# Forty of 48 activation tiles copied by DMA and transposed as float32r

## The chip, the cores and the metric

One core of one Trainium2 chip runs the kernel. The metric is the device time of one execution in microseconds, as the median of several runs. The engines named below: TensorE (PE in the profile; its loads of the stationary operand have a row of their own, PEld), VectorE (DVE), ScalarE (ACT), GpSimd (POOL) and the queue SP, from which most transfers are started. PSUM is the memory that TensorE writes into; a bank holds 128 x 512 float32.

## The reference

One decoder layer for 256 rows of 2048 channels in float32: attention over selected keys and a retention branch side by side, merged by sigmoid gates, then an MLP with a squared ReLU. Cut to what matters here:

```python
h = rms_norm(x, ln1_g[l])
aq, ak, av, iq, ik, iw, rq, rk, rv, rg, ga, gb = split(h @ w_in[l])
o_attn = dsa_attention(aq, ak, av, iq, ik, iw, topk)
y_ret = retention_chunkwise(rq, rk, rv, log_gamma)
o_ret = silu(rg) * group_norm_heads(y_ret, ret_gn_g[l], ret_gn_b[l])
merged = sigmoid(ga) * (o_attn @ w_up_attn[l]) + sigmoid(gb) * (o_ret @ w_up_ret[l])
x = x + merged @ w_out[l]
h2 = rms_norm(x, ln2_g[l])
x = x + square(relu(h2 @ w_ff1[l])) @ w_ff2[l]
```

The hidden width is 8192.

## The kernel before

**Products.** Every matrix product of size is made three times in float32r (`products`, L401 to L407): the rounded part of the activation with the rounded part of the weight, with the weight's rest, and the activation's rest with the rounded weight. So each operand exists as a pair of float32r tiles, `hi` and `lo`. For weights `split` makes the pair: ScalarE copies the raw tile into `hi` (L359), VectorE subtracts `hi` from the raw tile into `lo` (L360). For some weights VectorE first adds two raw tiles (L349). The stationary operand is the activation's, 128 x 128; the weights stream past it, 512 columns at a time.

**Order.** The whole work is a list of items, `use`, written ahead of time; one item is two K chunks of 128. In `run_block` and `second` (the second MLP product) an item is 12 products, in `first` (the sums of a fast block scheme for the gates and for the first MLP product) it is 6. `weights` starts loads up to 8 items ahead (1 MB each, on SP's queue) and splits 2 items ahead, in one case 3.

**Side work.** What has to be done beside the products are Python generators in the list `work`; each `step()` moves every one of them up to its next `yield`. `run_block` steps once for each K chunk, `first` and `second` once for each item. The instructions go into the engines' queues in that order, and each queue is worked off in order.

**Transposition.** Activations come out with rows on partitions and have to be turned before they can be a stationary operand. `transpose_in` (L432) waits a number of steps (the argument `wait`: 2, or `W_GN` = 7 for retention), takes a PSUM bank (`psum_t`, two of them in the first part, one in the MLP), has TensorE transpose four 128 x 128 blocks of a 128 x 512 tile into it (L438, with the float32 identity `ident`), and calls `split_into`: ScalarE copies the bank into `hi` (L429), VectorE subtracts into `lo` (L430). It is called 48 times:

- 8 times for the retention output (`normed`, L988): 4 blocks of 512 channels x 2 row tiles. VectorE's last operation before it is L987.
- 8 times for the merged tiles (L1043), blocks i = 0 to 3 x 2 row tiles; VectorE's L1042 makes the tile. Blocks 0 and 1 are the ones begun early over three quarters of K (`PAIR`, `PARTS`).
- 32 times for the MLP's activations (`hidden`, L1157), 8 groups of 1024 hidden channels x 2 halves x 2 row tiles. ScalarE makes ReLU (L1143) and square (L1144) into a staging tile.

In the groups 1 to 7 of the MLP, `merged(g)` interleaves the `first` items of group g with the `second` items of group g-1. `first` ends with `put`, which squares the tiles and calls `hidden`, after products 4 (two tiles), 5 and 6 (one each). The result of `second` is scaled by ScalarE (L1217) and added to a sum in memory by a DMA of GpSimd's queue (L1218).

**Staging tiles.** `stage()` gives a 128 x 512 float32 tile out of two rings: every fourth from a ring of 2, the others from a ring of 6. A tile whose slot is still in use makes its first writer wait.

Of the kernel before, what the change touches and what calls it, by code (L numbers as in the profile page):

```python
# [10 lines left out]
F32 = mybir.dt.float32  # L11
F32R = mybir.dt.float32r
I32 = mybir.dt.int32
AF = mybir.ActivationFunctionType
# [3 lines left out]
P = 128  # L18
# [4 lines left out]
BN = 512  # L23
# [10 lines left out]
FG = 8  # L34
NG = DFF // (FG * P)
# [124 lines left out]
def block_kernel(ctx, tc, cst, rot, xt, gains, w, x, ret_gn_g, ret_gn_b, out):  # L160
    nc = tc.nc
# [3 lines left out]
    cp = ctx.enter_context(tc.tile_pool(name="cp", bufs=1))  # L165
# [23 lines left out]


    W_NORM, W_SOFT, W_GN = 3, 5, 7
    n_stg, n_mid, n_sm = 8, {"ep": 12, "e4": 20}, 24
    late = {"ep": ep, "stg": ep}
    n_stage = [0]

    def nm(s):
        uid[0] += 1
        return f"{s}_{uid[0]}"

    def stage(shape=(P, BN)):  # L200
        n_stage[0] += 1
        pool, bufs = (late["stg"], 2) if n_stage[0] % 4 == 0 and "stg" in late else (sp, n_stg - 2)
        return pool.tile(list(shape), F32, tag="stg", name=nm("stg"), bufs=bufs)

    def mid(shape, dtype=F32):
        return late["ep"].tile(list(shape), dtype, tag="mid", name=nm("mid"), bufs=n_mid[late["ep"].name])

    def small(w):
        return sp.tile([P, w], F32, tag="small", name=nm("small"), bufs=n_sm)

    def psum_t():
        return PS["pt"].tile([P, BN], F32, tag="pt", name=nm("pt"))

    def psum_a():
        return PS["pa"].tile([P, BN], F32, tag="pa", name=nm("pa"))

    def act_pair(slot):
        a = ap[slot].tile([P, DK, 2, S], F32R, tag="act", name=nm("act"))
        return a[:, :, 0, :], a[:, :, 1, :], a

    work = []
# [19 lines left out]
    ident = csb[:, C_ID:C_ID + P]  # L241
    cmk = csb[:, C_CM:C_CM + P]


    warm = cp.tile([P, P], F32, name="warm")
    nc.vector.memset(warm, 0.0)
    wps = psum_a()
    for _ in range(11):
# [140 lines left out]
    def run_block(key, act, before=None, ps=None, k0=0, k1=None):  # L389
        nk, n = B[key]  # L390
        ps = ps or [PS["pm"].tile([P, BN], F32, tag="pm", name=nm("pm")) for _ in range(T)]
        for k in range(k0, k1 or nk):
            if k % HC == 0:
                ws = weights((key, k // KC, k % KC // HC))
            if before:
                before(k)
            step()
            products(ps, [p[:, :n] for p in (ws[0][:, k % HC], ws[1][:, k % HC])], [act(k, t) for t in range(T)], k == 0, k == nk - 1)
        return [p[:, :n] for p in ps]
# [9 lines left out]
    def of(a):  # L409
        return lambda k, t: tuple(z[:, k, t * P:(t + 1) * P] for z in a[:2])  # L410


    def rsqrt(v, n, mul):

        a, y, u = small(n), small(n), small(n)
        nc.vector.tensor_scalar(a, v, mul, EPS, op0=ALU.mult, op1=ALU.add)
        nc.vector.tensor_scalar(y.bitcast(I32), a.bitcast(I32), -0.5, float(0x5F3759DF), op0=ALU.mult, op1=ALU.add)
        for _ in range(3):
            nc.vector.tensor_tensor(u, y, y, op=ALU.mult)
            nc.vector.scalar_tensor_tensor(u, u, -0.5, a, op0=ALU.mult, op1=ALU.mult)  # L420
            nc.vector.scalar_tensor_tensor(y, u, 1.5, y, op0=ALU.add, op1=ALU.mult)
        return y

    def split_into(act, k0, nk, t, ps):

        src = ps.rearrange("p (c i) -> p c i", c=nk)
        hi = act[0][:, k0:k0 + nk, t * P:(t + 1) * P]
        lo = act[1][:, k0:k0 + nk, t * P:(t + 1) * P]
        nc.scalar.activation(hi, src, AF.Copy)  # L429
        nc.vector.tensor_tensor(lo, src, hi.bitcast(F32), op=ALU.subtract)  # L430

    def transpose_in(act, k0, t, src, wait=2):  # L432

        for _ in range(wait):
            yield
        ps = psum_t()
        for c in range(4):
            nc.tensor.transpose(ps[:, c * P:(c + 1) * P], src[:, c * P:(c + 1) * P], ident)  # L438
        split_into(act, k0, 4, t, ps)


# [32 lines left out]
    def evict(dst, ps, t, func=AF.Copy):  # L474
        nc.scalar.activation(dst, ps, func, scale=rows[t])
# [70 lines left out]
    for i in range(3):  # L546
        ps = run_block(("I", i), of(hT)) if i else psI
        for t in range(T):
            evict(iqs[:, t, i * IN:(i + 1) * IN], ps[t], t)
    mb = []  # L550

    def indexer():
        ik2 = mid([P, T, 2, ID])
# [70 lines left out]
    ps = run_block(("AV", 0), of(hT))  # L624
# [68 lines left out]
    for j in range(NKV):  # L693
        ps = run_block(("AQ", j), of(hT))
# [83 lines left out]
    def scaled(b):  # L778

        assert late["X2 made"]  # L780
        late["scaled"] = b + 1
        z = late["X2"][:, b // 2, b % 2 * 4:b % 2 * 4 + 4]
        hi, lo = (hT[a][:, 4 * b:4 * b + 4, P:] for a in range(2))
        nc.scalar.activation(hi, z, AF.Copy)
        nc.vector.tensor_tensor(lo, z, hi.bitcast(F32), op=ALU.subtract)

    for which, key in ((0, "RQ"), (1, "RK")):
        for i in range(2):
            last = (which, i) == (1, 0)
            ps = run_block((key, i), of(hT), before=(lambda k: scaled(k // 4 - 1) if k in (4, 8, 12) else None) if last else None)  # L790
# [93 lines left out]
    for gate, u in ((z, u) for z in BESIDE for u in range(2)):  # L884
# [10 lines left out]
        for item in beside(gate, u):  # L895
# [7 lines left out]
            else:  # L903
                branch(item, of(oT if gate == "GA" else hT))
                i = item[0][1] - 2 * u
# [13 lines left out]
    rT = act_pair(1)  # L919
# [28 lines left out]
    def retain(j, gb, rv, sg, am):  # L948
        for _ in range(2):
            yield  # L950
        ys = []
        for t in range(T):
            psy = psum_a()
            for a in range(2):
                c = slice(a * RV, (a + 1) * RV)
                for u in range(t + 1):
                    m = slice((a * (T - u) + t - u) * P, (a * (T - u) + t - u + 1) * P)
                    products([psy[:, c]], [v[:, c] for v in rv[u]], [[z[:, m] for z in am[u]]], u == 0, u == t)
            y = stage()
            nc.scalar.activation(y, psy, AF.Copy)  # L960
            ys.append(y)
            yield
        yield from normed(j, ys, gb, sg)

    def normed(j, ys, gb, sg):
        mv, vr, nb = small(4 * T), small(2 * T), small(2 * T)
        for t in range(T):
            for a in range(2):
                st = small(6)
                nc.vector.bn_stats(st, ys[t][:, a * RV:(a + 1) * RV])  # L970
                nc.vector.bn_aggr(mv[:, 4 * t + 2 * a:4 * t + 2 * a + 2], st)
        mean, var = (mv.rearrange("p (a b) -> p a b", b=2)[:, :, i] for i in range(2))
        nc.vector.tensor_copy(vr, var)
        yield
        r = rsqrt(vr, 2 * T, 1.0)
        nc.vector.scalar_tensor_tensor(nb, mean, -1.0, r, op0=ALU.mult, op1=ALU.mult)
        yield
        for t in range(T):
            y = ys[t]
            for a in range(2):  # L980
                c = slice(a * RV, (a + 1) * RV)
                i = 2 * t + a
                nc.scalar.activation(y[:, c], y[:, c], AF.Identity, scale=r[:, i:i + 1], bias=nb[:, i:i + 1])
            nc.vector.tensor_tensor(y, y, gb[0], op=ALU.mult)
            nc.vector.tensor_tensor(y, y, gb[1], op=ALU.add)
            yield
            nc.vector.tensor_tensor(y, y, sg[t], op=ALU.mult)  # L987
            work.append(transpose_in(rT, 4 * j, t, y, W_GN))  # L988

    for j in range(4):  # L990
        if j < 2:

            i = j
# [5 lines left out]
        for src in (ret_gn_g, ret_gn_b):  # L999
            g = mid([P, BN])  # L1000
            nc.gpsimd.dma_start(g, src[:, j * BN:(j + 1) * BN].to_broadcast([P, BN]))
            gb.append(g)
        for t in range(T):
            z = mid([P, BN])
# [6 lines left out]
        ps = run_block(("RV", j), of(hT))  # L1011
# [9 lines left out]
    mT = act_pair(0)  # L1021
    pair = {}
    def gates(i):
        ms = [mid([P, BN]) for _ in range(T)]
        for t, m in enumerate(ms):
            nc.gpsimd.dma_start(m, mgd[:, t, i * BN:(i + 1) * BN])
            nc.gpsimd.dma_start(sgb[:, t, i * BN:(i + 1) * BN], sgbd[:, t, i * BN:(i + 1) * BN])
        return ms
# [7 lines left out]
    for i in range(4):  # L1036
        ms = mss[i] if i in pair else gates(i)
        ps = run_block(("UR", i), of(rT), ps=pair.get(i), k0=len(PARTS[0]) * KC if i in pair else 0)
        for t, m in enumerate(ms):
            g = sgb[:, t, i * BN:(i + 1) * BN]  # L1040
            nc.vector.tensor_tensor(g, ps[t], g, op=ALU.mult)
            nc.vector.tensor_tensor(m, m, g, op=ALU.add)  # L1042
            work.append(transpose_in(mT, 4 * i, t, m))  # L1043


    x2 = px.tile([P, T, D], F32, tag="big2", name="x2")
# [62 lines left out]
    for i in range(4):  # L1109
        ps = run_block(("O", i), of(mT))  # L1110
        for t in range(T):
            z = x2[:, t, i * BN:(i + 1) * BN]
# [13 lines left out]
    hid = act_pair(0)  # L1126
# [26 lines left out]
    def form(f, k):  # L1153
        return tuple(xf[:, a, f, k, :] for a in range(2))

    def hidden(g, t, i):
        work.append(transpose_in([z[:, g % 2 * FG:] for z in hid[:2]], 4 * i, t, ys.pop((t, i))))  # L1157

    blocks = ((X11, X21), (X12, X22))
    ys = {}  # L1160
    for i in (1, 0):
        ps = run_block(("F1", i), lambda k, t: form(blocks[k // HK][t], k % HK))
# [107 lines left out]
```

## Time and profile before

| | |
|---|---|
| median of 3 runs | 1610.87 us (1610.86 to 1611.2) |
| the profiled execution | 1610.98 us |
| its span, first to last instruction | 1609.2 us |
| mean granted TensorE clock | 1.000 |
| DMA moved | 351.80 MB, 219 GB/s |
| transpositions in `transpose_in` | 192 |

A profile row of the form `L438 PE MATMUL pt<-csb,stg ... x160` names the line, engine, operation, the tile written and the tiles read, the shape and the count. The names are those of tiles: `pt` is the PSUM bank of transpositions, `csb` holds the identity, `stg` are staging tiles, `whi` and `wlo` the weights' pair, `act` the turned activations' pair, `pm`, `pq`, `pf`, `pa` the banks of products. Both float32 and float32r operands of TensorE stand there as f32. In the chain, a line gives start, length and what ran; in a timeline the bracket at the end is the engine's idle time just before and what ended it.

### The profile page before, as it was taken

The page shows a single profiled execution, that of the slowest core. Times are in us where ns is not written, and L with a number is a line of the kernel's source. Part 1 is how long each engine was busy: PE and PEld are TensorE (multiplying, and loading weights), DVE is VectorE, ACT ScalarE, POOL GpSimd, SP SyncE. Part 2 cuts the span into 40 slices and gives each one's busy share as a digit, 9 for nine tenths or more (in the row PEclk, how much of TensorE's full clock was granted, in tenths as well). Part 3 has the DMA queues.
Part 4 walks back from the last instruction along what each step waited for, and adds up shares of the span by engine and source line. Part 5 has one row for each costly group of instructions (what it writes and reads, how often), then busy time and mean ns, then how long its engine had stood idle before and what let it go on. Part 6 is the DMA issues. An engine that isn't in the chain of part 4 may idle for free.

```text
span 1609.2 us, 19815 instructions
## 1 busy us (share of the span) xinstructions
PE 1603.2 (100%) x7438; PEld 1334.0 (83%) x7438; DVE 1308.5 (81%) x1466; ACT 1011.1 (63%) x1316; POOL 90.7 (6%) x135
## 2 busy tenths in 40 slices
PE   9999999999999999999999999999999999999999
PEld 8978888888888888888888888888888888888887
DVE  6678779898989898688665589898989898989884
ACT  7556666566566666455444666767767676767672
POOL 0000000000000001202000000000000000000000
PEclk9999999999999999999999999999999999999999
DMA  9645346656565655857556574767676777777773
GB/s 330 220 150 183 132 148 247 222 215 234 198 253 209 262 200 184 320 199 261 183 206 255 203 276 142 250 195 255 207 251 197 242 225 235 235 236 233 217 200 134
DMA packets 68416, 351.80 MB, mean 219 GB/s; under 512 B 7776, under 2 KB 14560, under 8 KB 32736
## 3 DMA queue, kind: packets, MB, share of 16 engines
q1 hardware_dynamic: 51040, 308.96, 52.6%
q0 software_dynamic: 14256, 35.14, 10.0%
q10 hardware_dynamic: 3024, 6.44, 1.1%
q8 instruction: 58, 0.95, 0.2%
q14 instruction: 38, 0.31, 0.1%
HBM read 323.24 MB, written 27.26 MB: 218 GB/s over the span
## 4 chain that ended last, share of the span: by engine, by line
PE 98%; DVE 1%; DMA 0%; ACT 0%; issue 0%; ACTq 0%; DVEq 0%
PE pm L407 12%; PE pm L406 12%; PE pm L405 12%; PE pf L405 11%; PE pf L407 11%; PE pf L406 11%; PE pq L406 9%; PE pq L405 9%; PE pq L407 9%; PE pt L438 1%; PE pa L405 1%; PE pa L407 0%; PE pa L406 0%; PE pt L532 0%; PE pt L681 0%; PE pa L940 0%
## 5 line engine op out<-in xcount | busy, mean ns | idle before, releaser
L360 DVE TENSOR_TENSOR wlo<-raw,whi 128x1024 fp32r<-128x1024 f32 (+2 forms) x544 | 646.3, 1201 | 214.8 <-ACT whi L359 205.3
L359 ACT ACTIVATE whi<-raw 128x1024 fp32r<-128x1024 f32 (+2 forms) x544 | 563.7, 1043 | 403.0 <-PE pm L407 193.2
L405 PE MATMUL pm<-whi,act 128*128 128x512 f32 (+1 forms) x800 | 310.0, 388 | 0.6 <-ACT act L449 0.6
L406 PE MATMUL pm<-wlo,act 128*128 128x512 f32 (+1 forms) x800 | 307.0, 384 | 0.5 <-DVE wlo L360 0.5
L407 PE MATMUL pm<-whi,act 128*128 128x512 f32 (+1 forms) x800 | 307.5, 384 | 0.0
L405 PE MATMUL pf<-whi,act 128*128 128x512 f32 (+1 forms) x768 | 298.7, 390 | 0.0
L406 PE MATMUL pf<-wlo,act 128*128 128x512 f32 (+1 forms) x768 | 298.4, 389 | 0.0
L407 PE MATMUL pf<-whi,act 128*128 128x512 f32 (+1 forms) x768 | 298.3, 388 | 0.0
L360 DVE TENSOR_TENSOR wlo<-rawc,whi 128x1024 fp32r<-128x1024 f32 x176 | 215.0, 1222 | 43.5 <-ACT whi L359 41.3
L359 ACT ACTIVATE whi<-rawc 128x1024 fp32r<-128x1024 f32 x176 | 186.4, 1059 | 81.2 <-PE pf L407 35.7
L349 DVE TENSOR_TENSOR raw<-raw,raw 128x2048 f32<-128x2048 f32 x88 | 201.2, 2287 | 1.3 <-DMA raw<-in_w_dram 0.6
L407 PEld LDWEIGHTS pm<-whi,act 128*128 128x128 f32 x800 | 150.5, 188 | 27.8 <-DVE act L450 0.2
L406 PEld LDWEIGHTS pm<-wlo,act 128*128 128x128 f32 x800 | 150.6, 188 | 26.9 <-DVE wlo L360 1.3
L405 PEld LDWEIGHTS pm<-whi,act 128*128 128x128 f32 x800 | 150.4, 188 | 26.9 <-ACT act L449 0.8
L405 PEld LDWEIGHTS pf<-whi,act 128*128 128x128 f32 x768 | 144.1, 188 | 30.1 <-ACT whi L359 0.8
L407 PEld LDWEIGHTS pf<-whi,act 128*128 128x128 f32 x768 | 144.3, 188 | 29.8
L406 PEld LDWEIGHTS pf<-wlo,act 128*128 128x128 f32 x768 | 144.3, 188 | 29.4
L405 PE MATMUL pq<-whi,xf 128*128 128x512 f32 x392 | 154.4, 394 | 0.0
L407 PE MATMUL pq<-whi,xf 128*128 128x512 f32 x392 | 152.9, 390 | 0.0
L406 PE MATMUL pq<-wlo,xf 128*128 128x512 f32 x392 | 152.7, 390 | 0.0
L1218 POOL DMA_DIRECT2D sums<-ev x56 | 48.2, 942 | 777.0 <-ACT ev L1217 775.3
L407 PEld LDWEIGHTS pq<-whi,xf 128*128 128x128 f32 x392 | 73.6, 188 | 15.4
(210 smaller groups left out, 1531.2 us busy)
## 6 DMA issues: line engine op xcount, KB each, us to landing
raw<-in_w_dram SPq DMA_DIRECT2D x188, 1024.0 KB, 5.3
rawc<-in_w_dram SPq DMA_DIRECT2D x88, 1024.0 KB, 5.8
sums<-ev POOLq DMA_DIRECT2D x56, 256.0 KB, 5.4
raw<-in_w_dram SPq DMA_DIRECT2D x8, 736.0 KB, 4.8
raw<-in_w_dram SPq DMA_DIRECT2D x7, 512.0 KB, 7.0
raw<-in_w_dram SPq DMA_DIRECT2D x8, 368.0 KB, 7.3
stg<-in_x_dram SPq DMA_DIRECT2D x8, 256.0 KB, 7.7
rqkd<-stg POOLq DMA_DIRECT2D x8, 256.0 KB, 2.7
```

Source lines behind the costliest of these rows:

```text
L349: nc.vector.tensor_tensor(one, one, two, op=ALU.add)
L359: nc.scalar.activation(a, src, AF.Copy)
L360: nc.vector.tensor_tensor(b, src, a.bitcast(F32), op=ALU.subtract)
L405: nc.tensor.matmul(d, h, hi, start=first, stop=False, skip_group_check=skip)
L406: nc.tensor.matmul(d, h, lo, start=False, stop=False, skip_group_check=skip)
L407: nc.tensor.matmul(d, l, hi, start=False, stop=last, skip_group_check=skip)
L438: nc.tensor.transpose(ps[:, c * P:(c + 1) * P], src[:, c * P:(c + 1) * P], ident)
L1218: nc.gpsimd.dma_start(sums[:, t, i * BN:(i + 1) * BN], z, accum_op=ALU.add)
```

## The change

`stage` can now give a float32r tile. `moved(src)` takes one and copies a finished 128 x 512 float32 tile into it by a DMA of ScalarE's queue, bit by bit (the destination is seen as float32). `transpose_in` turns a float32r tile with a float32r identity, `unit`, into the same PSUM bank seen as float32r, and any other tile as before. Retention's 8 calls, the 4 calls for merged blocks 0 and 1, and the 28 calls for the MLP's groups 0 to 6 go through `moved`; the 4 calls for merged blocks 2 and 3 and the 4 of the last MLP group stay as they are. The moved ones wait 10 steps (retention, merged tiles, half 1 of group 0) or 6 (the rest of the MLP), where they waited 7 and 2.

```diff
+    W_MOVED, W_EARLY = 6, 10
...
-    def stage(shape=(P, BN)):
+    def stage(shape=(P, BN), dtype=F32):
         n_stage[0] += 1
         pool, bufs = (late["stg"], 2) if n_stage[0] % 4 == 0 and "stg" in late else (sp, n_stg - 2)
-        return pool.tile(list(shape), F32, tag="stg", name=nm("stg"), bufs=bufs)
+        return pool.tile(list(shape), dtype, tag="stg", name=nm("moved" if dtype == F32R else "stg"), bufs=bufs)
+
+    def moved(src):
+
+        z = stage(dtype=F32R)
+        nc.scalar.dma_start(z.bitcast(F32), src)
+        return z
...
+    unit = cp.tile([P, P], F32R, name="unit")
...
+    def turn(ps, c, src, i):
+
+        d, z = ps[:, c * P:(c + 1) * P], src[:, i * P:(i + 1) * P]
+        if src.dtype == F32R:
+            nc.tensor.transpose(d.bitcast(F32R), z, unit)
+        else:
+            nc.tensor.transpose(d, z, ident)
+
     def transpose_in(act, k0, t, src, wait=2):
...
-            nc.tensor.transpose(ps[:, c * P:(c + 1) * P], src[:, c * P:(c + 1) * P], ident)
+            turn(ps, c, src, c)
...
+    nc.scalar.activation(unit, ident, AF.Copy)
...
-            work.append(transpose_in(rT, 4 * j, t, y, W_GN))
+            work.append(transpose_in(rT, 4 * j, t, moved(y), W_EARLY))
...
-            work.append(transpose_in(mT, 4 * i, t, m))
+            work.append(transpose_in(mT, 4 * i, t, *((moved(m), W_EARLY) if i < 2 else (m,))))
...
     def hidden(g, t, i):
-        work.append(transpose_in([z[:, g % 2 * FG:] for z in hid[:2]], 4 * i, t, ys.pop((t, i))))
+        y = ys.pop((t, i))
+        src = (moved(y), W_EARLY if i > 2 * g else W_MOVED) if g < NG - 1 else (y,)
+        work.append(transpose_in([z[:, g % 2 * FG:] for z in hid[:2]], 4 * i, t, *src))
```

## The prediction

> **What bounds the kernel now.** I read the page first: the busy shares, then the chain that ended last, by engine and by line.
>
> ```profile
> span 1609.2 us, 19815 instructions
> PE 1603.2 (100%) x7438; PEld 1334.0 (83%) x7438; DVE 1308.5 (81%) x1466; ACT 1011.1 (63%) x1316; POOL 90.7 (6%) x135
> ...
> PE 98%; DVE 1%; DMA 0%; ACT 0%; issue 0%; ACTq 0%; DVEq 0%
> ```
>
> TensorE works from end to end and 98% of the chain is TensorE. So a nanosecond taken out of TensorE's stream comes off the time, as long as no other engine falls behind. Next the transposition line, L438, and the table of waits for the weight loads.
>
> ```profile
> L438 PEld LDWEIGHTS pt<-csb,stg x160: 137/140/144, 690.7 to 1561.3; 128*128 128x128 f32 x160
> L438 PE MATMUL pt<-csb,stg x160: 269/272/328, 690.9 to 1561.4; 128*128 128x128 f32 x160
> L438 PE MATMUL pt<-csb,mid x32: 271/272/301, 789.8 to 841.4; 128*128 128x128 f32 x32
> ...
> PEld pt L438 <- ACT stg L1144: 1.9, 7, 0.4
> ...
> PEld pq L406 <- DVE wlo L360: 1.1, 4, 0.4
> ```
>
> 192 transpositions, four to a call. The 272 ns is the length of one from entry to exit, and they overlap; what one costs the stream has to be read from the chain in order of time (start, length, what).
>
> ```profile
> 145.52 0.89 PE pa L662 x8
> ...
> 668.49 0.86 PE pa L940 x4
> ...
> 673.29 0.12 PE pa L405
> 673.41 0.12 PE pa L406
> ...
> 690.87 0.23 PE pm L407
> 691.10 0.44 PE pt L438 x4
> 691.54 0.23 PE pm L405
> ...
> 1119.51 0.49 PE pt L438 x4
> ...
> 1122.08 0.44 PE pt L438 x4
> ```
>
> Four float32 transpositions hold the stream 0.44 us, 0.110 each. L662 is a plain float32 product of 128 columns and its records cost the same, 0.89/8 = 0.111; L940 with 256 columns costs 0.86/4 = 0.215. So a float32 record costs by its columns, 0.84 ns for each. The float32r products cost 0.12 at 256 columns and 0.23 at 512 (L405): 0.45 to 0.47 ns a column, about half.
>
> **Which transpositions change, counted from the code.** Retention output: 4 blocks x 2 row tiles = 8 calls. Merged tiles: blocks 0 and 1, 4 calls. MLP activations: 7 groups x 4 = 28. Together 40 calls, 160 transpositions; the last group and merged blocks 2 and 3 keep float32.
>
> **What a float32r transposition costs.** No row shows one, nor any float32r product of 128 columns. Two things can set it. The columns: half of the 0.12 is 0.060; a line through 0.12 and 0.23 also gives about 0.065; I take 0.064. The load of its 128x128 operand: here the timeline of the weight loads (start, length, line), and two rows by line with the mean and the median of one load in ns.
>
> ```profile
> 1119.34 0.14 PEld L438 LDWEIGHTS pt<-csb,stg 128*128 128x128 f32 x1 [0.25 <-ACT stg L1144]
> ...
> 1119.34 0.20 PEld L438 LDWEIGHTS pt<-csb,stg 128*128 128x128 f32 x2 [0.25 <-ACT stg L1144]
> ...
> 1119.73 0.19 PEld L405 LDWEIGHTS pq<-whi,xf 128*128 128x128 f32 x1
> 1119.84 0.19 PEld L406 LDWEIGHTS pq<-wlo,xf 128*128 128x128 f32 x1
> ...
> L405 PEld LDWEIGHTS pm<-whi,act 128*128 128x128 f32 x800 | 150.4, 188 | 26.9 <-ACT act L449 0.8
> ...
> L940 PEld LDWEIGHTS pa<-rqT,rk x32: 187/190/193, 665.4 to 722.0; 128*128 128x128 f32 x32
> ```
>
> In the answers for two narrow windows the first load of a transposition alone ends after 0.14 and two together after 0.20: the second began 0.06 after the first. An ordinary load of the main products is longer (0.19) and the next comes 0.11 behind it. So a transposition's load occupies 0.06, an ordinary one 0.11, where nothing hides them. Bounds for the float32r transposition: from below 0.06 (both columns and load), from above 0.11 (an ordinary load, or columns that go at the float32 rate). I take 0.064, since the short load (140 ns) goes with the transposition in these rows, not with the type: a plain float32 product (L940) has the long load of the float32r products, 190 and 188.
>
> **A call.** After the fourth transposition the next main product needs an ordinary load, 0.11, that can start only when the fourth has its operand in the array. With float32 this is hidden, because the fourth lasts 0.110 anyway. With float32r the fourth slot stays 0.11. So a call is 3 x 0.064 + 0.11 = 0.302 against 0.44: 0.138 saved. 40 x 0.138 = **-5.5 us**. At the lower end, with all four at 0.06: 40 x 0.20 = -8.0. At the upper end 40 x 0 = 0; I see nothing that would make the transposition itself longer than the float32 one of the same columns.
>
> In a sentence aside: the Trainium skill's page "TensorE: Matmul & The Clock Gate", section "Back-to-back issue gap", gives about 81 ns for each pair of weight load and 128-column matmul in a stream; by it the sum would be 160 x (110 - 81) = -4.6 us, an estimate from that page, and no run here shows the pair.
>
> **The waits of the weight loads on L1144** (the second ReLU step on ScalarE) go, because the transposition comes four steps later. The 1.9 us in the table is idle time of the loader; what it costs is the difference between the two calls in the chain, 0.49 - 0.44 = 0.05. Seven times: **-0.3 us**. Late next could be the copy, so its timing decides.
>
> **The copies.** 40 DMAs of 256 KB on ScalarE's queue. The nearest rows:
>
> ```profile
> DMA packets 68416, 351.80 MB, mean 219 GB/s; under 512 B 7776, under 2 KB 14560, under 8 KB 32736
> ...
> sums<-ev POOLq DMA_DIRECT2D x56, 256.0 KB, 5.4
> ...
> sums<-x ACTq DMA_DIRECT2D x8, 256.0 KB, 3.1
> ...
> out_dram<-stg ACTq DMA_DIRECT2D x7, 256.0 KB, 2.7
> ...
> L1116 ACTq DMA_DIRECT2D sums<-x x8: 326/330/611, 862.0 to 930.9; - x8
> ...
> DMA to landing us min/median/max: 2.3/3.1/4.5
> ```
>
> Issue 0.33, landing 3.1, at worst 4.5 on this queue. A step of a `first` item is 6 products, 6 x 0.23 = 1.4 us, of a `second` item 12, 2.8 us. An activation waits for 6 steps where it waited for 2. After product 4 the four extra steps are three of 1.4 and one of 2.8: 7.0 us; after products 5 and 6 the same. One call in each group has no margin now (it is the one that waits for L1144), so it gets 7.0 - 0.33 - 4.5 = 2.2 us to spare at the worst landing. Cost 0. If landing took 5.4, the accumulating writes' median, 1.3 would be left. The users of the transposed tiles come later still: the last activation of a group is transposed four items before the `second` item that reads it, three of 1.4 and one of 2.8, 7.0 us ahead, and its split needs an eviction on ScalarE and one on VectorE, 0.59 + 0.69. Retention goes from 7 to 10 steps of 1.4: 4.2 more, beside what the 7 leave now; its last block has 24 steps of the partial `UR` products before the drain. The merged tiles have 10 steps, in a block of 16 or the two of 4 ahead of it.
>
> The transfer load: 40 x 256 KB read and written on top of 351.80 MB moved is 3% of bytes. The weights come on SP's queue, up to 8 items ahead. Cost 0; POOL's queue gets nothing new.
>
> **ScalarE's queue.** Each copy is issued in order on ScalarE, 0.33 us, 13 us in all, and waits for its source. For the MLP the source is ScalarE's own square; behind the waiting issue stand the splits (L359), behind these VectorE's L360, then TensorE. For retention (8) and merged tiles (4) the source is a VectorE product, and ScalarE stands until VectorE gets there. The tightest place is the stretch after product 4, here in ScalarE's timeline (idle before in brackets), behind two groups of the tile evictions and ahead of the merged tiles' end at 788:
>
> ```profile
> L429 ACT ACTIVATE act<-pt x48: 573/587/600, 691.6 to 1562.8; 128x512 fp32r<-128x512 f32 x48
> ...
> L430 DVE TENSOR_TENSOR act<-pt,act 128x512 fp32r<-128x512 f32 x48 | 32.5, 685 | 0.8 <-ACT act L429 0.4
> ...
> 1116.00 0.63 ACT L1143 ACTIVATE stg<-stg 128x512 f32<-128x512 f32 x1
> 1116.66 0.63 ACT L1144 ACTIVATE stg<-stg 128x512 f32<-128x512 f32 x1
> 1117.20 0.62 ACT L1143 ACTIVATE stg<-stg 128x512 f32<-128x512 f32 x1
> 1117.72 1.05 ACT L359 ACTIVATE whi<-raw 128x1024 fp32r<-128x1024 f32 x1
> ...
> 1122.55 0.60 ACT L429 ACTIVATE act<-pt 128x512 fp32r<-128x512 f32 x1 [0.76 <-PE pt L438]
> ...
> 1129.39 1.06 ACT L359 ACTIVATE whi<-raw 128x1024 fp32r<-128x1024 f32 x1 [0.66 <-PE pf L407]
> ...
> 1135.29 1.06 ACT L359 ACTIVATE whi<-rawc 128x1024 fp32r<-128x1024 f32 x1 [1.66 <-PE pf L407]
> ...
> 787.97 1.28 DVE L1042 TENSOR_TENSOR mid<-mid,sgb 128x512 f32<-128x512 f32 x2
> 789.98 1.06 ACT L359 ACTIVATE whi<-raw 128x1024 fp32r<-128x1024 f32 x1 [1.66 <-PE pm L407]
> ```
>
> From 1116.00 to 1128.7, where its 0.66 of idle before the row at 1129.39 begins, no row of ScalarE's timeline waits over 0.8, so 2 x 0.33 of issue delays the next split there by up to 0.66. But the same change takes two evictions of transposed tiles out of this stretch (L429 and L430, 2 x 0.59 on ScalarE, 2 x 0.69 on VectorE with their means above) and puts them about 7 us later, where ScalarE waits 1.66 us for TensorE between splits. VectorE is the fuller of the two, so I expect a net of about zero. For the merged tiles VectorE ends L1042 at 789.25, and the split behind waited until 789.98 for TensorE: two issues fit. I put **+0.6 us** for all of it: twelve copies behind VectorE at 0.05, the step that a late operand cost in the chain. Bounds: -1.1 (the table's four waits of L406 on wlo go, because VectorE is relieved) to +13 (every issue shows on TensorE).
>
> Staging slots: a group takes eight instead of four, which is the ring of 6 + 2, so a slot comes back one group later; cost 0. The copy of the identity in float32r is one small ScalarE instruction.
>
> **Sum.** -5.5 - 0.3 + 0.6 = -5.2 on a span of 1609.2: 1604.0. The profiled execution took 1610.98, 1.78 more than its span, and lies 0.11 above the median of 1610.87. So 1604.0 + 1.78 - 0.11 = **1605.7**. A measurement of this kernel tells about 0.2%, 3.2 us, from no change.
>
> **Rivals.**
> - *Nothing gained (1611).* The float32r operand is loaded like an ordinary one, 0.11, or streams at 0.110. For it: both ordinary types have loads of 188 to 190 ns, the transposition's 140 is known for float32 alone. Against it: the short load is already there for a 4-byte type. 1610.9, or up to 1611.5 with the 0.6. The Trainium skill, same page, section "Part 4: PE-mode transpose", says that a transposition's time (about 275 ns in a kernel) is mostly operand access latency; by that the type would not matter. The trace's 272 ns agrees as a length, but the chain charges 110.
> - *Slower.* ScalarE stands at the copies (wait for the own square to drain, 0.33 of issue, then the split), and the lead of two splits runs out at product 4. It decides once a copy costs TensorE over 0.138 us; if each of the 40 costs its whole 0.33, +13.2 - 5.8 = +7.4, 1618. For it: the 12 us with hardly a gap. Against: ScalarE is 63% busy, and most splits wait 1.66 for TensorE.
> - *Partly eaten (1607.9).* The same mechanism at the 14 copies after product 4 alone, at 0.2 each: -5.8 + 2.8 = -3.0, within what can't be told.
>
> **How the numbers follow.** Forecast 0.68, nothing gained 0.12, partly eaten 0.07, slower 0.13. Faster takes the first: 0.68 (with the lower end -8.0 in it); same 0.19; slower 0.13. Range: below, -8.0 with the waits, without a loss, is 1602.6, of which little is left out at 1603.0; above, 1611.5 takes in no gain and leaves out the slower case. The forecast's own range is 1603.0 to 1607.5.
>
> **What would show it.** In the chain of the changed kernel a float32r call should read 0.29 to 0.32 where a float32 one reads 0.44; the load rows 140 ns, not 188. No wait of L438's successor on L1144, nor on the copy. New rows of `moved` on ScalarE's queue with 0.33 and landing near 3. ScalarE busy as before, and its splits late by less than 0.7 after product 4. The prediction is wrong if a call still reads 0.44, or if waits of the main products on L359 or L360 appear beyond the few tenths of now.

## The result and the profile after

The changed kernel takes 1622.73 us (median of six runs, 1619.77 to 1623.42), the kernel before 1610.88 in the same session (1610.81 to 1611.2). The ratio is 1.007, 95% interval 1.0059 to 1.0081: slower by 0.7%, where 0.3% faster was forecast, and outside the range of 1603.0 to 1611.5. The profiled execution took 1623.42 on a span of 1621.6, so the span grew by 12.4 us.

In the changed file the lines named here stand 8 to 19 lower: the products are L413 to L415, the split of weights L367 and L368, the addition of raw tiles L357, the split of turned tiles L437 and L438, the float32r transposition L444, the float32 one L446, the copy L209, ReLU and square L1160 and L1161. First the page: span, busy times, shares of the chain.

```profile
span 1621.6 us, 19886 instructions
PE 1602.2 (99%) x7438; PEld 1331.8 (82%) x7438; DVE 1307.2 (81%) x1466; ACT 1012.3 (62%) x1317; POOL 90.7 (6%) x135
...
PE 92%; DMA 3%; DVE 2%; ACT 1%; issue 1%; ACTq 0%; DVEq 0%
```

TensorE's busy time hardly moved (1603.2 to 1602.2), and ScalarE's neither. What is new is the DMA in the chain, 3%, where it had 0%. The table of waits (who waits for whom: us in total, times, longest) names it:

```profile
PE pt L444 <- DMA moved<-stg: 11.5, 6, 2.7
...
PE pf L414 <- DVE wlo L368: 1.0, 1, 1.0
...
PEld pt L446 <- ACT stg L1161: 0.3, 1, 0.3
```

TensorE stands six times at a float32r transposition until the copy that feeds it has landed: once in each of the groups 1 to 6. In the groups 2 to 6 it is the first tile of product 4; in group 1 it is the tile of product 5, whose copy is issued at 1042.16 and lands 9.8 later. Measured from the start of the last product to the start of the transposition, the six gaps are 1.17, 2.45, 2.61, 3.07, 2.48 and 2.06 us. An ordinary gap is 0.23; and a call behind a wait takes 0.05 longer than the others (0.34 instead of 0.29, as it has nothing to overlap with). So the six cost 13.84 - 6 x 0.23 + 6 x 0.05, about **12.8 us**. The chain in order of time (start, length, what) shows the second of them:

```profile
1120.23 6.88 DMA moved<-stg
1127.11 0.14 issue
1127.24 0.50 PE pt L444 x4
...
1128.57 0.43 PE pq L413
...
1133.54 0.29 PE pt L444 x4
1133.83 0.30 PE pq L413
```

The copy is issued at 1120.23 and lands 6.88 later. Two more things are to be seen here. Behind this wait the products stand 0.43 apart and not 0.23, for 3.4 us; the row by window below has a granted clock of 0.50 there. That costs another **1.6 us**. In this execution it happened at this one wait, not at the longer ones of 2.61 and 3.07. And a later call, whose copy was in time, takes 0.29, with 0.30 for the next product where 0.23 is usual: 0.37 against 0.444 before.

Two other delays stand in this execution. One is 1.2 us at the start of group 1, where a main product waits for its weight's split; the chain there:

```profile
980.24 0.25 PE pq L414
...
980.54 0.59 issue
981.13 1.23 DVE wlo L368
...
982.41 0.50 PE pf L414
```

In VectorE's timeline an addition of two raw tiles (L357, 2.29 us from 978.92) stands ahead of that split; in the runs without the delay that addition stands behind the split. The other is 0.9 us at 330.8, long before the first copy, in this execution alone. The account: saved by shorter calls 3.1 (34 single calls at 0.075, three pairs that follow each other at 0.172; the waits counted apart), saved by the vanished waits on the square 0.35; lost 12.8 + 1.6 + 1.2 + 0.9. That makes +13.0 against +12.4 measured.

**Why the copies are late.** The copy's own line, over the MLP's stretch (ns min/median/max; the last row is us from issue to landing):

```profile
L209 ACTq DMA_DIRECT2D moved<-stg x24: 472/472/624, 1033.6 to 1487.3; - x24
DMA to landing us min/median/max: 2.3/6.9/9.8
```

And the DMA issues of two windows, 1120.2 to 1121.5 and 1145 to 1146, with the median landing in the last column:

```profile
moved<-stg ACTq DMA_DIRECT2D x2, 256.0 KB, 7.1
...
moved<-stg ACTq DMA_DIRECT2D x1, 256.0 KB, 2.3
```

The same 256 KB land in 2.3 or in 7.1. What differs is what else the DMA engines do; by windows, each from issue to landing of a copy (the last three columns are granted clock, DMA share and GB/s; the row of 1128.30 is the slow clock from above):

```profile
687.11:689.41 2.30, 2.30 (x12) 1.91 (x11) 1.46 (x2) 1.06 (x1) 0.00 (x0) 1.00 0.58 150
1145.04:1147.34 2.30, 2.30 (x12) 1.90 (x11) 2.30 (x2) 1.11 (x2) 0.00 (x0) 1.00 0.71 281
1120.23:1127.13 6.90, 4.95 (x22) 3.75 (x20) 6.87 (x6) 5.24 (x6) 1.72 (x2) 1.00 0.97 357
...
1042.16:1051.96 9.80, 9.16 (x43) 7.24 (x41) 8.02 (x9) 7.48 (x9) 1.71 (x2) 1.00 1.03 341
...
1128.30:1131.70 3.40, 3.40 (x9) 2.65 (x8) 1.35 (x3) 1.89 (x4) 0.00 (x0) 0.50 1.01 334
```

Where the copy lands in 2.3 the engines are busy 58 to 71%; where it takes 7 to 10, they are full. Before the change the same view gives these means, for the place that the prediction's landing came from (L1116, 862 to 931) and for the MLP:

```profile
860.00:935.00 75.00, 74.99 (x344) 61.80 (x343) 44.32 (x68) 44.36 (x69) 0.00 (x0) 1.00 0.59 211
1025.00:1500.00 475.00, 475.00 (x2140) 392.58 (x2139) 426.32 (x350) 335.33 (x384) 37.87 (x44) 1.00 0.71 225
```

A mean over the MLP (0.71 before, 0.74 after) hides stretches at 0.97. SP's queue shows what fills them (start, and the loads that it issues; the length of a row with several runs from the first issue to the end of the last):

```profile
1118.64 0.33 SPq L335 DMA_DIRECT2D rawc<-in_w_dram  x1
1120.84 8.33 SPq L335 DMA_DIRECT2D raw<-in_w_dram  x3
```

And ScalarE's timeline with its issues:

```profile
1117.58 0.63 ACT L1161 ACTIVATE stg<-stg 128x512 f32<-128x512 f32 x1
...
1119.58 0.62 ACT L1161 ACTIVATE stg<-stg 128x512 f32<-128x512 f32 x1
...
1120.23 1.12 ACTq L209 DMA_DIRECT2D moved<-stg  x2
```

Three weight loads of 1 MB run beside the first copy: the one issued at 1118.64, which is still on its way, and two of the row below it, issued at 1120.84 and 1125.43 (its third comes after the landing). The accumulating writes of GpSimd's queue begin only at 1126.5. The first packet of the copy moves 2.5 us after the issue, where it is 1.1 in the quiet window at 1145. The loads go in packets of 8 KB, the copies in packets of 2 KB; from 1122.5 to 1126, while both run, the copies get, by the packets in the trace, 28 to 44 KB in half a microsecond and the loads 104 to 176.

The second half of the cause is the lead. From the issue at 1120.23 TensorE needs only 22 products (the window's 4.95 us) to stand at the transposition. The lead is 4.9, the landing 6.9, the wait 2.1 by the timeline. ScalarE's timeline shows one thing more: the square of the first tile is over at 1118.21, but its copy goes out only at 1120.23, behind the second tile's square, because `put` makes both squares before it calls for the copies. That is 2.0 us of lead, about as much as is missing; no run tried a copy right behind its own square.

### The profile page after: what moved, and what is told of

Same layout as the page of the kernel before. It is cut to its first block, busy times and chain, and to the rows that moved or that the text cites. A ratio compares the mean times of both kernels' runs of the same rounds, so it can differ in the third digit from the quotient of the medians.

```text
span 1621.6 us, 19886 instructions
## 1 busy us (share of the span) xinstructions
PE 1602.2 (99%) x7438; PEld 1331.8 (82%) x7438; DVE 1307.2 (81%) x1466; ACT 1012.3 (62%) x1317; POOL 90.7 (6%) x135
## 4 chain that ended last, share of the span: by engine, by line
PE 92%; DMA 3%; DVE 2%; ACT 1%; issue 1%; ACTq 0%; DVEq 0%
PE pm L413 11%; PE pm L415 11%; PE pm L414 11%; PE pf L413 10%; PE pf L414 10%; PE pf L415 10%; PE pq L413 8%; PE pq L414 8%; PE pq L415 8%; DMA moved<-stg 3%; DVE wlo L368 1%; PE pt L444 1%; ACT whi L367 1%; DVE stg L858 1%; PE pa L413 1%
## 5 line engine op out<-in xcount | busy, mean ns | idle before, releaser
L368 DVE TENSOR_TENSOR wlo<-raw,whi 128x1024 fp32r<-128x1024 f32 (+2 forms) x544 | 644.7, 1200 | 219.6 <-ACT whi L367 212.4
L367 ACT ACTIVATE whi<-raw 128x1024 fp32r<-128x1024 f32 (+2 forms) x544 | 563.0, 1043 | 404.6 <-PE pm L415 191.9
L413 PE MATMUL pm<-whi,act 128*128 128x512 f32 (+1 forms) x800 | 309.2, 387 | 0.7 <-ACT act L465 0.7
L415 PE MATMUL pm<-whi,act 128*128 128x512 f32 (+1 forms) x800 | 307.2, 384 | 0.0
L413 PE MATMUL pf<-whi,act 128*128 128x512 f32 (+1 forms) x768 | 298.8, 390 | 0.0
L415 PE MATMUL pf<-whi,act 128*128 128x512 f32 (+1 forms) x768 | 298.3, 388 | 0.0
L368 DVE TENSOR_TENSOR wlo<-rawc,whi 128x1024 fp32r<-128x1024 f32 x176 | 214.8, 1221 | 51.5 <-ACT whi L367 48.5
L367 ACT ACTIVATE whi<-rawc 128x1024 fp32r<-128x1024 f32 x176 | 186.4, 1059 | 86.2 <-PE pf L415 37.0
L357 DVE TENSOR_TENSOR raw<-raw,raw 128x2048 f32<-128x2048 f32 x88 | 201.1, 2286 | 2.3 <-DMA raw<-in_w_dram 1.6
L415 PEld LDWEIGHTS pm<-whi,act 128*128 128x128 f32 x800 | 150.5, 188 | 27.6 <-DVE act L466 0.2
L413 PEld LDWEIGHTS pm<-whi,act 128*128 128x128 f32 x800 | 150.3, 188 | 27.5 <-ACT act L465 0.9
L415 PEld LDWEIGHTS pf<-whi,act 128*128 128x128 f32 x768 | 144.5, 188 | 29.8
L413 PEld LDWEIGHTS pf<-whi,act 128*128 128x128 f32 x768 | 144.4, 188 | 29.9 <-ACT whi L367 0.5
L413 PE MATMUL pq<-whi,xf 128*128 128x512 f32 x392 | 154.4, 394 | 0.0
L415 PE MATMUL pq<-whi,xf 128*128 128x512 f32 x392 | 153.1, 390 | 0.0
L415 PEld LDWEIGHTS pq<-whi,xf 128*128 128x128 f32 x392 | 73.7, 188 | 15.5
```

Of the source, the lines that this page charges most:

```text
L357: nc.vector.tensor_tensor(one, one, two, op=ALU.add)
L367: nc.scalar.activation(a, src, AF.Copy)
L368: nc.vector.tensor_tensor(b, src, a.bitcast(F32), op=ALU.subtract)
L413: nc.tensor.matmul(d, h, hi, start=first, stop=False, skip_group_check=skip)
L415: nc.tensor.matmul(d, l, hi, start=False, stop=last, skip_group_check=skip)
```

## The experiments

All ratios are against the kernel before, with 95% intervals. E1 to E4, E5 and E6, and E7 to E9 ran in three sessions, each with runs of the kernel before beside them; the last was on another chip.

**E1. More steps for product 4's tiles.** All tiles of half 1 wait 10 steps, not only those of group 0.

```diff
-        src = (moved(y), W_EARLY if i > 2 * g else W_MOVED) if g < NG - 1 else (y,)
+        src = (moved(y), W_EARLY if i else W_MOVED) if g < NG - 1 else (y,)
```

> The tiles of product 4 (half 1) wait 10 steps in every group where they wait 6 in the changed kernel; nothing else differs. Theory L (the copy lands late: issue to landing about 7 us there, the transposition stands only about 4.9 us behind the issue): the six waits of TensorE (0.99 to 2.89 us, 12.8 in all) and the halved clock behind one of them (1.6) go, 1622.7 falls to 1607 to 1609. Theory S (the issues on ScalarE hold up the splits): the number and place of the issues are the same, so it stays at 1619 or above. Theory O (VectorE's queue stands in another order): 1609 to 1612, with waits of main products on L368.

Measured 1609.69 (1609.41 to 1609.96), ratio 0.9992 [0.9983, 1.0001]: no difference from before, but 13 us better than the change. The waits on the copy are gone, also the one at product 5's tile of group 1, whose steps E1 leaves alone: there the copy landed in 9.3 and the transposition stood 9.5 behind its issue (9.8 and about 9.0 in the change). The two copies after product 4 land as late as ever (DMA issues, landing in the last column):

```profile
moved<-stg ACTq DMA_DIRECT2D x2, 256.0 KB, 7.2
```

What remains at the transposition, in the table of waits, is a wait for the bank:

```profile
PEld pt L444 <- DVE act L438: 2.9, 11, 0.4
```

So the landing is not the loss in itself; the lead that is shorter than the landing is. With 10 steps the calls of a group follow each other by 3.1 us, and the later one finds the MLP's only bank still being emptied by L438. All calls, each with what it adds to the product behind it, sum to 19.37 us against 21.94 before, 2.6 saved; of it the delay at 980 (present here too) eats 1.2. That leaves 1.4, which is what was measured against before in its session.

**E2. float32r without the copy.** The last writer of the tile writes it as float32r, and the steps are those of before. The values that are turned are rounded to float32r, and their rests are zero; this leaves out the exact copy, and shows the price of the transposition alone.

```diff
     def moved(src):
-        z = stage(dtype=F32R)
-        nc.scalar.dma_start(z.bitcast(F32), src)
-        return z
+        return stage(dtype=F32R)
...
-        nc.scalar.activation(y, y, AF.Square)
-        return y
+        z = moved(y) if g < NG - 1 else y
+        nc.scalar.activation(z, y, AF.Square)
+        return z
...
```

> float32r transposition without any copy: the last writer (square, or VectorE's product and sum) rounds into the float32r tile, so the turned values have float32r precision and their rest is zero; steps to wait as before the change. Theory L, with the call measured in the changed kernel (0.369 against 0.444, pairs 0.707 against 0.879): 34 x 0.075 + 3 x 0.172 = 3.1 less than before, 1607.8. By the prediction's 0.138 a call: 1605.4. If float32r brings nothing: 1610.9. Theory S: as L, since no issue is left.

Measured 1608.18 (1607.81 to 1608.95), ratio 0.9982 [0.9973, 0.999]: 2.9 us faster than before. A call costs 0.369 with a pace of 0.083 for each transposition. All calls sum to 18.95 us, 3.0 less than before. That is the whole worth of the type here: about 3 us, not 5.5.

**E3. The copies with the float32 transposition.** Copies and steps as in the change, but into float32 tiles.

```diff
-        z = stage(dtype=F32R)
-        nc.scalar.dma_start(z.bitcast(F32), src)
+        z = stage()
+        nc.scalar.dma_start(z, src)
```

> Copies, slots and waits as in the changed kernel, but float32 transpositions. Theory L: the waits for the copies stay, the 3.1 of the transposition is lost: 1624.5 to 1627. Theory S says the same sum but with waits of the main products on L367 and L368 instead of waits on the copy. If the late copy were no cause: 1611 to 1613.

Measured 1626.0 (1624.43 to 1626.79), ratio 1.0092 [1.0078, 1.0106]. The table of waits:

```profile
PE pt L446 <- DMA stg<-stg: 10.3, 5, 2.9
```

And the chain at the place shown above:

```profile
1120.19 6.72 DMA stg<-stg
```

Five of the six waits, at the same places, without any float32r (of group 1's, 0.10 is left): the loss belongs to the copies. By the medians it is 3.3 us above the change: about what the type is worth, though not cleanly so, since the clock was halved twice here (at 1127.4 and 1301.5) and once in the profile of the change.

**E4. The steps alone.** No copy, float32, but the waits of 6 and 10 steps.

```diff
-        z = stage(dtype=F32R)
-        nc.scalar.dma_start(z.bitcast(F32), src)
-        return z
+        return src
```

> The steps to wait alone (10 and 6), without copies and in float32. Theory L: within 0.5 of before, less 0.3 for the waits on the square: 1610.3 to 1611.0. Theory O (the later evictions reorder VectorE's queue): 1 to 2 us above before, with a wait of a main product on L368 near the start of group 1.

Measured 1610.53 (1610.18 to 1610.79), ratio 0.9997 [0.9988, 1.0006]. The steps take the waits on the square away (all calls sum to 21.59 us, 21.94 before) and cost nothing that the runs can tell; the delay at 980 is absent.

**E5. Weight loads in small rows.** In the MLP each load of 1 MB becomes four DMAs of 2 KB rows, so that its packets have the copies' size.

```diff
-            nc.sync.dma_start(r[:, :, :n], src)
+            if key[0][0] == "F2" or (key[0][0] in QUARTERS and isinstance(key[0][1], int)):
+                for c in range(KC):
+                    nc.sync.dma_start(r[:, c, :n], src[:, c, :])
+            else:
+                nc.sync.dma_start(r[:, :, :n], src)
```

> The changed kernel, but every weight load of the MLP groups is issued as four DMAs of 256 KB with rows of 2 KB instead of one of 1 MB with rows of 8 KB; the copies keep their rows of 2 KB. Theory L1 (the 16 engines take turns between the queues by packets, so a copy beside loads of four times its packet gets a fifth of the engines): the copies after product 4 land in 3.5 to 5 us instead of 7, the waits of TensorE on the copy fall from 11.5 to under 4 us, and the time to 1609 to 1615. Theory L2 (a late copy is a matter of bytes in the queues ahead of it, whatever their packets): landing stays at 6 to 8 us, waits and time as in the changed kernel, 1620 to 1624. A rival for both: the loads themselves get late with the small rows, which would show as waits of L367 or L357 on raw.

Measured 1610.72 (1609.73 to 1612.41), ratio 0.9999 [0.999, 1.0008]. The waits on the copy are gone. The DMA issues of the two copies after product 4, at 1119.02:

```profile
moved<-stg ACTq DMA_DIRECT2D x2, 256.0 KB, 4.4
```

And the line of the copy over the whole MLP (us, min/median/max):

```profile
DMA to landing us min/median/max: 2.6/5.6/8.9
```

After product 4 the landing fell from 7.1 to 4.4 (the middle of 2.7 and 6.1), but at the products 5 and 6 it rose: to 7.2 to 8.9 at product 5 in the groups 2 to 6 (4.6 to 8.0 in the change) and to 5.3 to 5.8 at product 6 (2.3 to 3.5). And the loads stand at other moments than in the change: a load had just ended when the first copy began. So this agrees with a share that goes by the packet, but does not separate it from the moments of the loads. New waits appeared as well, of the split on the weights (13.9 us in 10 on ScalarE, 3.0 in 4 in the change); whether they cost time can't be told, as the runs spread over 2.7 us.

**E6. More steps, spaced.** Half 1 waits 10 and 12 steps for the two row tiles, and half 0 of group 0 is not moved.

```diff
-        src = (moved(y), W_EARLY if i > 2 * g else W_MOVED) if g < NG - 1 else (y,)
+        src = (moved(y), W_EARLY + 2 * t if i else W_MOVED) if g < NG - 1 and (g or i) else (y,)
```

> The half-1 tiles wait 10 (first row tile) and 12 steps (second), so that the second need not wait for the one bank of transpositions; the two tiles of half 0 of group 0 stay float32 without a copy, as before the change. Theory L plus the measured price of a call: 158 less two calls, 3.0 saved, the 0.15 a group for the bank and the 1.2 us at the start of group 1 are gone: 1607.5 to 1608.5, the best of all so far except the one without copies. If the 1.2 us at the start of group 1 was not due to group 0's copies: 1608.5 to 1609.5.

Measured 1608.34 (1608.0 to 1609.37), ratio 0.9984 [0.9974, 0.9993]. The delay at 980 is gone, the wait for the bank is halved in number (table of waits):

```profile
PEld pt L444 <- DVE act L438: 2.0, 6, 0.3
```

**E7. The copies on SP's queue.** Nothing else is changed: the copies stand in line with the weight loads.

```diff
-        nc.scalar.dma_start(z.bitcast(F32), src)
+        nc.sync.dma_start(z.bitcast(F32), src)
```

> The changed kernel with its 40 copies issued on SP's queue, among the weight loads, and not on ScalarE's. Theory L (the copy is late because the 16 engines are full with weight loads in flight beside it): on SP's queue a load that comes after the copy cannot take from it, so the copies after product 4 land in 3 to 5 us and the waits on the copy fall below 4 us of the 11.5; 1609 to 1616. SP, which now waits for each square before it goes on to the next load, may make loads late: then waits of L367 on raw take their place, and the time can go up to 1625. If the landing has nothing to do with the loads: 7 us and 1620 to 1624 as before.

Measured 1606.66 (1606.29 to 1608.76), ratio 0.9974 [0.9965, 0.9984]: the best kernel of this study, 4.4 us faster than before. SP's queue around the two copies after product 4:

```profile
1117.41 0.33 SPq L335 DMA_DIRECT2D rawc<-in_w_dram  x1
1118.99 1.12 SPq L209 DMA_DIRECT2D moved<-stg  x2
1120.20 5.35 SPq L335 DMA_DIRECT2D raw<-in_w_dram  x2
```

Their landing, by the DMA issues:

```profile
moved<-stg SPq DMA_DIRECT2D x2, 256.0 KB, 4.3
```

The transposition in the chain:

```profile
1123.96 0.29 PE pt L444 x4
```

And the window from the issue to 1123.00 (DMA share and GB/s at the end):

```profile
1118.99:1123.00 4.01, 4.01 (x19) 3.31 (x19) 4.01 (x5) 3.03 (x4) 0.07 (x1) 1.00 1.00 380
```

The lead is the same as in the change (4.97 us from issue to transposition), the steps are the same, and the DMA engines are just as full (1.00). But the copies stand ahead of the next loads in one queue and land in 4.3, so nothing waits. All calls sum to 18.47 us against 21.94: 3.5 saved of the 4.4 gained; what the other 0.9 is stays open. The queue alone does not make a copy fast: after product 5, with loads ahead of them in it, the copies landed in 6.6 to 7.6 here, without a wait, since the lead is longer there.

**E8. The copies on GpSimd's queue.** A queue of their own beside the loads, as in the change, but not ScalarE's.

```diff
-        nc.scalar.dma_start(z.bitcast(F32), src)
+        nc.gpsimd.dma_start(z.bitcast(F32), src)
```

> The changed kernel with its 40 copies issued on GpSimd's queue. Theory L: another queue, the same engines and the same loads beside them: landing again 6 to 9 us, the six waits stay, 1620 to 1628. Theory S (ScalarE's issues hold up its splits): no issue is left on ScalarE, so it falls to 1608 to 1612.

Measured 1612.64 (1612.03 to 1613.55), ratio 1.0011 [1.0002, 1.002]. Six waits again, at half the length, now all at the first tile of product 4, groups 1 to 6 (table of waits):

```profile
PE pt L444 <- DMA moved<-stg: 5.0, 6, 1.3
```

The two copies after product 4, by the DMA issues:

```profile
moved<-stg POOLq DMA_DIRECT2D x2, 256.0 KB, 6.1
```

And the chain there:

```profile
1117.62 5.29 DMA moved<-stg
...
1123.05 0.51 PE pt L444 x4
```

The lead is no longer than in the change: TensorE has 4.7 us of work from the issue to the transposition (4.9 there). The copy lands in 5.3 instead of 6.9. So the queue beside the loads is still too slow for this lead, but less so than ScalarE's, by 1.6 us. The result lies between what the theories expected.

E8 changed more than the queue. The page's table of queues has packets, MB and share; the first two lines are from before (q10 is ScalarE's queue, q0 GpSimd's), the third from the change, the fourth from E8:

```profile
q0 software_dynamic: 14256, 35.14, 10.0%
q10 hardware_dynamic: 3024, 6.44, 1.1%
...
q10 hardware_dynamic: 8784, 16.93, 2.8%
...
q0 software_dynamic: 17456, 45.62, 11.5%
```

The copies' 10.5 MB are 5760 packets on ScalarE's queue and 3200 on GpSimd's; in the traces their bulk goes in packets of 2 KB there and of 4 KB here. Beside the loads, about as many packets of the copies as of the loads pass in half a microsecond, in the change (14 to 22 beside 13 to 22) and in E8 (16 to 20 beside 14 to 16); by that the larger packets would be the reason. But in E5, where both have packets of 2 KB, the copy after product 5 (issued at 1127.85) got 128 packets beside 504 of the loads, a fifth. So why the two queues differ is not settled.

**E9. Eight steps.** Half 1 of the groups 1 to 6 waits 8 steps.

```diff
-        src = (moved(y), W_EARLY if i > 2 * g else W_MOVED) if g < NG - 1 else (y,)
+        src = (moved(y), (W_EARLY if i > 2 * g else W_MOVED + 2) if i else W_MOVED) if g < NG - 1 else (y,)
```

> The tiles of product 4 wait 8 steps, two more than in the changed kernel (one item of 6 products and one of 12, 4.1 us). Theory L: the transposition then stands 4.9 + 4.1 = 9 us behind the issue and the copies land after 6.9 to 7.5, so the six waits go as with 10 steps: 1608.5 to 1610.5. If more than the landing is wrong: above 1613.

Measured 1608.94 (1608.65 to 1609.39), ratio 0.9987 [0.9978, 0.9997]. The copies after product 4, issued at 1118.65, land as in the change (DMA issues):

```profile
moved<-stg ACTq DMA_DIRECT2D x2, 256.0 KB, 7.0
```

The transposition comes 9.1 us behind their issue and waits for nothing, in the chain:

```profile
1127.79 0.29 PE pt L444 x4
```

Two steps more, on ScalarE's queue and with the slow landing, turn +11.9 us into -2.1. All calls sum to 18.54, 3.4 saved; the delay at 980, 1.2, is still there.

## Why the prediction was wrong

**The copies, "cost 0": this step failed, in both its terms.** The landing of 3.1, at worst 4.5, came from the eight copies at 862 to 931, where the engines were busy 59%. After product 4 three weight loads run beside, and the copies took 7.1. The prediction did look at 5.4, the median of GpSimd's writes, and found 1.3 to spare; but that rested on the second term, the extra lead of 7.0 us from four steps. It was 4.9. The call without a margin before stood at the transposition as soon as the square was made, 33 products (7.3 us) after product 4, and it now stands there after 54 (12.1 us, without the wait): 21 products more, 4.8 us, where four steps were taken for 30, 7.0 us. The four steps are right, but `merged` puts one more `second` item behind product 4, so the two steps of before were two `second` items, 24 products, and the call already stood 9 products (2.0 us) behind its step; now it stands exactly at its sixth. That margin of before was counted twice. With a lead of 4.9 even 5.4 would have waited, as E8's 5.3 did. E1 and E9 show the lead to be what decides (same landing, more lead, no wait), E7 the landing (same lead, shorter landing, no wait), E3 that the type has no part in it, and E4 that the steps have none.

**The halved clock and the order at 980** were not in the prediction: 1.6 and 1.2 us. The first follows from the waits, though not from each. In the records of the granted clock it changes only at whole multiples of 3.41 us. On that grid TensorE stood idle, in the one stretch just before a halving, for 2.06 us in the change, 1.90 and 2.70 in E3 and 1.96 in E7 (at its very start). In no other stretch of the eleven traces, the end of the program left out, was it idle for more than 1.71. The wait of 2.45 fell whole into one stretch, less its ordinary step; the longer ones were divided between two, 1.09 and 1.59, 1.37 and 0.85. These are four cases read from traces, and no run was made to test them. The delay at 980 depends on how VectorE's queue comes out, which the change shifts (it is in the change, E1, E3, E5 and E9, not in E2, E4, E6, E7, E8).

**The price of a call: mechanism right, size off.** 0.302 was forecast, 0.369 measured, so 0.075 is saved and not 0.138. The loads of the float32r transpositions, by line (ns min/median/max):

```profile
L444 PEld LDWEIGHTS pt<-unit,moved x160: 137/139/145, 697.0 to 1496.9; 128*128 128x128 f32 x160
```

Three of them in the loader's timeline:

```profile
1133.38 0.31 PEld L444 LDWEIGHTS pt<-unit,moved 128*128 128x128 f32 x3
```

And two calls in a row in the chain, 0.63 for eight:

```profile
965.99 0.63 PE pt L444 x8
```

The short load of 139 ns goes with the transposition, as was argued; that rival ("nothing gained") is dead. The exposed ordinary load of 0.11 behind the fourth is there too (0.37 = 3 x 0.083 + 0.12). What failed is the 0.064 for a transposition. It came from the columns and from one spacing of 0.06 between a call's first two loads. Three loads take 0.31, so their mean spacing is (0.31 - 0.14) / 2 = 0.085: the first spacing is not the steady one. That the loads and not the columns bind the stream is a reading of this: the loads stand as far apart as the transpositions, 0.083, where the columns alone would have given 0.06; no run varies one without the other. The Trainium skill, page "TensorE: Matmul & The Clock Gate", section "Back-to-back issue gap", gives about 81 ns for a pair of load and 128-column matmul. The trace agrees with that, with 83, and the sum by it (-4.6) was nearer than mine of -5.5 to the 3.0 that 40 x 0.075 make. The same page of the Trainium skill, section "Part 4: PE-mode transpose", by which the type would not matter, comes near for the length of one (247 ns against 272) but not for what it costs the stream (0.083 against 0.110).

**The waits on the square** went, as forecast: of the seven one is left, of the last group, which is not moved. -0.35 against -0.3.

**ScalarE's queue: right that it costs next to nothing,** though an issue takes 0.47 and not 0.33. Main products wait on L367 no more than they did on L359 before (0.5 us against 0.8), and ScalarE is as busy as before. So the rival "slower", 1618, had the sign and nearly the size but not the mechanism: not ScalarE stands at the copies, but TensorE at their landing. Its own condition (a copy that costs TensorE over 0.138 us) was met on the average: 12.8 over 40 copies is 0.32 each, though six copies alone cost it.

**What stays open:** whether the copies' small share beside the loads comes from the packet size, for which E8's packets speak and against which E5's do; whether a copy issued right behind its own square, 2.0 us sooner, would have been in time without more steps; and 0.9 of the 4.4 us that E7 gained.

## What to carry to other kernels

A copy's landing time is a property of the stretch in which it runs: take it from transfers between the same neighbours, and not from the mean or from a quiet place. The DMA share of those few microseconds warns, but does not give the number. A copy in the middle of a dependency needs either a lead beyond its worst landing (two steps more were enough here) or a place in the queue of the big loads, ahead of the next of them. And count a lead from the place where the consumer really stands in its engine's queue, not from the step that the code names.

## What was not expected of the hardware

The same copy of 256 KB landed in 2.3 us at a DMA share of 0.6 to 0.7, and in 7 to 10 us at a full one; but at the same full share it took 4.3 in the queue of the loads, 6.1 in GpSimd's and 7.1 in ScalarE's. A float32r transposition of 128x128 costs the stream 0.083 us, a float32 one 0.110, though the float32r products of wider operands go at half the float32 price. Behind one wait of 2.45 us TensorE's clock stood at 0.50 for 3.4 us, and not behind one of 3.07 that was divided between two of the clock's stretches of 3.41 us.
